# Forward substitution of the 16x16 triangular blocks issued by GpSimd (RWKV-7 + mLSTM hybrid layer)

## The chip, the cores and the metric

One core of a Trainium2 chip runs the whole program. Its engines are TensorE (PE, with its weight loads as PEld), VectorE (DVE), ScalarE (ACT), GpSimd (POOL) and SyncE (SP); each takes its instructions strictly in program order and waits at the head of its own queue until the semaphores of that instruction are there. The metric is the device time of one execution in microseconds, as the median of several runs.

## What is computed

One inference step of a decoder layer: RMSNorm, one projection `u @ w_in`, an RWKV-7 branch and an mLSTM branch on it, a gated merge, an output projection and a squared-ReLU MLP. 1024 new prompt tokens (with 16 meta tokens ahead of them, 1040 rows) and 8 running sequences of 8 tokens each go through it. The part that matters here is the RWKV-7 recurrence over 8 heads of width 64:

```python
def _rwkv7_step(S, inp):
    r, w, k, v, kk, a = inp
    sa = jnp.einsum('bhvk,bhk->bhv', S, -kk)
    S = S * w[:, :, None, :] + sa[..., None] * (kk * a)[:, :, None, :] + v[..., None] * k[:, :, None, :]
    return S, jnp.einsum('bhvk,bhk->bhv', S, r)
...
    S_T, y = lax.scan(_rwkv7_step, S0.astype(F32), (tm(r), tm(decay), tm(k), tm(v), tm(kk), tm(a)))
```

The kernel does it in chunks of 64 tokens. Within a chunk the step written with `sa` becomes a unit lower triangular 64x64 system for each head, and its inverse is needed. The inverse is built from the diagonal 16x16 blocks outwards: those blocks are inverted by forward substitution, and the blocks beside the diagonal follow by small matmuls.

## The kernel before

The program runs in stages. From about 85 to 880 us of the span it is in the RWKV stage: 24 steps (4 pairs of heads j, 6 groups g of 3 chunks). One step works on 2 heads x 64 tokens = 128 partitions and 3 chunks. A step is cut into four stages, and the program is pipelined over the steps: while stage a of step i runs, stage b of step i-1, stage c of step i-2 and stage d of step i-3 run beside it.

- Stage a makes the decays and the chunk matrices: rho (L654 to L656), `wa` and the running sum of log decays `cc` (L669, L672), products on GpSimd (L673, L684 to L687: RB and the middle part of KB), `bda` on VectorE (L682), the chunk matmuls L697, their masking X1 (L699), and the diagonal blocks `nd` (L703, L705). `nd` goes through DRAM to the tile NR by two DMAs (L709), which lays the 16x16 blocks out by row.
- Stage b starts with the forward substitution. L754 sets x to the identity; then, for n = 15 down to 1, L757 makes tmp = NR column * x column and L759 adds it to the remaining columns: 30 elementwise instructions of 128x3xn elements, each needing the one before it. L761 spreads x into the block diagonal XC, L764 transposes it, and the matmuls L769 to L798 with their evictions follow; L801 (ScalarE) and L802 (VectorE) write the result ATb.
- Stage c carries the state: L811, L814 and L815 (PE) read ATb, L822 and L823 make GH, L826 and L827 make MR, and then chunk after chunk PE's L885 (c = GH x Vs) and VectorE's L893 (next Vs = decay * c) wait for each other; L841 makes the outputs. One step of six also has the sample part (L853 to L923).
- Stage d is the group norm of the outputs (L938 to L953; L613 is on GpSimd, `newton`, L173 to L181, on VectorE).

Between the stages' matmuls PE runs filler: the projection matmuls L277, L279 and L281 of `Block.run`, 72 of them for each unit, which `pull(n)` places at points of a table. The tables (ORDER, ORDER_A, ORDER_B: stage letter, matmuls to pull) fix what `run_step` records. PE's order is kept as recorded (`manual_schedule`); the order of VectorE, ScalarE and GpSimd in this stage is set by the scheduler of the framework when the program is built, so it changes when instructions are given to another engine. The filler's weights are split in two parts: ScalarE casts `hi` (L199) and GpSimd makes `lo` = raw - hi (L201, 128x1024).

Of the kernel before, what the change touches and what calls it, by code (L numbers as in the profile page):

```python
# [12 lines left out]
ALU = mybir.AluOpType  # L13
# [16 lines left out]
G = 3  # L30
# [71 lines left out]
def tile_hybrid_trunk_step(ctx, tc, x_prompt, x_sample, st_S, st_shift, st_C, st_n, st_m, st_conv,  # L102
# [23 lines left out]
    def bank(nm):  # L126
        return PS["pool"].tile([128, 512], F32, tag=nm, name=nm, bufs=PS[nm])
# [20 lines left out]
    V = nc.vector  # L148
    PO = nc.gpsimd
# [5 lines left out]
    K = {k: (Cl[:, a:a + n] if k in LATE else Ct[:, a - NL:a - NL + n]) for k, (a, n) in OFF.items()}  # L155
# [213 lines left out]
    with banks(s=4, m=2), ExitStack() as st:  # L369
# [7 lines left out]
        for i in range(9):  # L377
            xt = xp.tile([128, D], F32, tag="xt", name="xt", bufs=9)
            n = 128 if i < 8 else 80
# [236 lines left out]
    def tl(n, sh=(GC,), bufs=1):  # L616
        return gp.tile([128] + list(sh), F32, tag=n, name=n, bufs=bufs)

    def hmm(o, l, r_, **kw):
        for s in HP:  # L620
            mm(o[s], lhsT=l[s], rhs=r_[s], **kw)
# [128 lines left out]
    def stage_b(j, g, st):  # L750
        X1, NR = st["X1"], st["NR"]
        x = tl("x", (G, 16))
        tmp = tl("tmp", (G, 16))
        V.tensor_copy(out=x, in_=K["xi"].unsqueeze(1).broadcast_to([128, G, 16]))  # L754
        for s in range(15):
            n = 15 - s
            V.tensor_tensor(out=tmp[:, :, :n], in0=NR[:, s + 1:16, :, s].rearrange("p t c -> p c t"),  # L757
                            in1=x[:, :, s:s + 1].broadcast_to([128, G, n]), op=ALU.mult)
            V.tensor_tensor(out=x[:, :, s + 1:16], in0=x[:, :, s + 1:16], in1=tmp[:, :, :n], op=ALU.add)  # L759
        XC, QC, XT = tl("XC", (G, 64)), tl("QC", (G * 32,)), tl("XT", (G, 64))  # L760
        V.tensor_tensor(out=XC.rearrange("p c (b t) -> p c b t", b=4), in0=x.unsqueeze(2).broadcast_to([128, G, 4, 16]),  # L761
                        in1=K["m16"].rearrange("p (b t) -> p b t", b=4).unsqueeze(1).broadcast_to([128, G, 4, 16]), op=ALU.mult)
        odd = lambda ap: ap.rearrange("p (b d) -> p b d", d=32)[:, :, 16:]
        V.transpose(out=XT, in_=XC)  # L764
        yield
        ps = bank("b")
        for c in range(G):
            for s in HP:
                mm(ps[s, 32 * c:32 * c + 32], lhsT=X1[s, c, 128:192], rhs=odd(XC[s, c]), start=True, stop=True)  # L769
        p4 = lambda t_: t_.rearrange("p (c b d) -> p c b d", c=G, d=16)  # L770
        V.tensor_tensor(out=p4(QC), in0=p4(ps[:, :32 * G]), in1=odd(K["mw32"]).unsqueeze(1).broadcast_to([128, G, 2, 16]), op=ALU.mult)
        yield
        ps = bank("b")
        for c in range(G):
            hmm(ps[:, 32 * c:32 * c + 32], XT[:, c], QC[:, 32 * c:32 * c + 32], start=True, stop=True)
        xv = XC.rearrange("p c (b d) -> p c b d", d=32)[:, :, :, 16:]
        V.tensor_tensor(out=xv, in0=p4(ps[:, :32 * G]), in1=xv, op=ALU.add)
        V.transpose(out=XT, in_=XC)
        for h, s in enumerate(HP):
            nc.scalar.copy(out=bd["x"][s, :, h, :], in_=XC[s])  # L780
        yield
        ps = bank("b")
        for c in range(G):
            for s, q in zip(HP, HQ):
                mm(ps[q, 32 * c:32 * c + 32], lhsT=X1[s, c, 128:160], rhs=XC[s, c, 32:], start=True, stop=True)
        for i, q in enumerate(HQ):
            V.tensor_copy(out=QZ[q], in_=ps[q, :32 * G])
        yield
        ps = bank("b")
        for c in range(G):  # L790
            for s, q in zip(HP, HQ):
                mm(ps[q, 32 * c:32 * c + 32], lhsT=XT[s, c, :32], rhs=QZ[s, 32 * c:32 * c + 32], start=True, stop=True)
        for h, q in enumerate(HQ):
            V.tensor_copy(out=bd["x"][q, :, h, 32:], in_=ps[q, :32 * G].rearrange("p (c d) -> p c d", c=G))
        yield
        ps = bank("b")
        for c in range(G):
            mm(ps[:, 128 * c:128 * c + 128], lhsT=flat(bd["x"][:, c]), rhs=X1[:, c, 0:128], start=True, stop=True)  # L798
        pv = ps[:, :128 * G].rearrange("p (c a t) -> p c a t", c=G, a=2)
        at = ATb.rearrange("p c a h t -> p c (a h) t")  # L800
        nc.scalar.copy(out=at[HP[0], :, 0::3], in_=pv[HP[0]])  # L801
        V.tensor_copy(out=at[HP[1], :, 1:3], in_=pv[HP[1]])  # L802
        yield
# [179 lines left out]
    for i in range(NS + 3):  # L983
        gens = {}
        for x, f, d in (("d", stage_d, 3), ("c", stage_c, 2), ("b", stage_b, 1)):
            if 0 <= i - d < NS:
                k = steps[i - d]
                gens[x] = f(*k, sts[k], SS_) if x == "c" else f(*k, sts[k])
        if i >= NS:
            run_step(gens, ORDER, 72 * (i < NS + 2), i == NS + 1)  # L990
            continue
        j, g = steps[i]
        if g == 0 and j:
            mix_all()
            queue.pop(0)
            run_step(gens, ORDER, 72)
            blocks(0)
            mix_all()
            queue.pop(0)
            run_step({"a": stage_a(j, g, sts[j, g])}, ORDER_A, 72 * FILLS[0])  # L1000
        else:
            gens["a"] = stage_a(j, g, sts[j, g])
            run_step(gens, ORDER_A if i == 0 else ORDER_B if i == 1 else ORDER, 72 * (FILLS[g] + (g == 5) * (1 if j == 3 else 2)), g == 1 and j > 0)
            while g == 5 and j < 3 and (live or queue[0]):
                pull(1)
                drain()
# [139 lines left out]
    for a, n in U_TILES:  # L1146
# [4 lines left out]
        for r_, T_, c in ((0, IG, 0), (32, FG, 1)):  # L1151
# [22 lines left out]
                    in1=MT[:, 15:15 + SEQ].rearrange("p (c t) -> p c t", t=128)[:, :, 0:1].broadcast_to([4, 8, 128]), op=ALU.add)  # L1174
# [4 lines left out]
    for c0 in (0, 5):  # L1179
        ps = sbank()  # L1180
        for c in range(c0, c0 + 5):
            a, n = CH[c]
            nc.tensor.transpose(ps[:n, 68 * (c - c0):68 * (c - c0) + 68], E2[:, a:a + n], ident[:68, :68])
        for c in range(c0, c0 + 5):
            a, n = CH[c]
# [660 lines left out]
```

## Time and profile before

| | before |
|---|---|
| median of 3 runs | 2103.38 us (2100.62 to 2105.63) |
| profiled execution: span from first to last instruction | 2102.9 us (0.5 us under the median of the runs; its own device time is not listed apart) |
| mean granted TensorE clock | 0.971 |
| RWKV stage, 100 to 880 us: PE / DVE / ACT / POOL busy | 708.0 / 609.9 / 269.5 / 174.0 us of 780 |
| L757, L759, L754 on DVE, whole span | 97.5 + 81.5 + 4.2 us |

Busy time is the time in which an engine executes; waiting at a semaphore is not counted. A row of the timeline gives the start in us, the duration in us, engine, line, operation, output and inputs with their shapes, and in brackets the idle time ahead of it on its engine with what ended it. A row of grouped lines ends with busy us, mean ns of one, and idle us ahead of the group's instructions.

One round of six steps (one pair of heads) takes some 198 us; the six steps between 281.9 and 479.7 us take 26.6, 32.0, 27.6, 27.1, 35.05 and 49.45 us. They are called A to F below, in this order; the last two have more filler.

### The profile page before, as it was taken

What the parts mean: (1) busy time and instruction counts of PE and PEld (TensorE: products, weight loads), DVE (VectorE), ACT (ScalarE), POOL (GpSimd) and SP (SyncE); (2) the same over time, 40 slices, a digit from 0 to 9 for tenths busy, and PEclk for the clock granted to TensorE, in tenths of its full rate; (3) what the DMA queues carried; (4) which work ended last, traced back from release to release, by engine and by line L of the source; (5) the groups of instructions that cost most, each with busy time, mean ns of one, the idle gap of its engine ahead of it and who ended that gap; (6) DMA issues with size and microseconds to landing.
All of it is one profiled execution on the core that took longest, in us unless ns stands there. A gap on an engine that the chain in (4) does not pass through costs nothing.

```text
span 2102.9 us, 32130 instructions
## 1 busy us (share of the span) xinstructions
PE 1974.6 (94%) x12325; PEld 1788.6 (85%) x12325; DVE 1364.2 (65%) x3503; ACT 704.7 (34%) x1654; POOL 511.1 (24%) x392
## 2 busy tenths in 40 slices
PE   8989898999989899989899997999999999999996
PEld 8978788888888788889888886988889999998895
DVE  6478778877887888578776639624444444445447
ACT  7333333333334333254654323331112222222122
POOL 2322122212222222122432404221112212112125
PEclk9999999999999999999999999999999999999998
DMA  5221111212111112231656614211111111111114
GB/s 162 62 68 54 46 52 57 64 45 66 55 51 49 52 61 66 64 107 62 230 175 200 215 60 145 71 51 41 41 41 41 50 51 41 51 41 43 49 32 164
DMA packets 148491, 161.59 MB, mean 77 GB/s; under 512 B 20429, under 2 KB 121607, under 8 KB 148337
## 3 DMA queue, kind: packets, MB, share of 16 engines
q1 hardware_dynamic: 148336, 159.54, 23.7%
q8 instruction: 97, 1.59, 0.3%
q14 instruction: 58, 0.47, 0.1%
HBM read 121.98 MB, written 37.27 MB: 76 GB/s over the span
## 4 chain that ended last, share of the span: by engine, by line
PE 48%; DVE 12%; ACT 2%; DMA 2%; issue 2%; POOL 1%; DVEq 0%; SPq 0%; ACTq 0%; POOLq 0%
PE g L215 11%; PE g L213 11%; PE g L214 11%; PE g L281 2%; PE g L277 2%; PE g L279 2%; PE g L1719 1%; DVE acc L1097 1%; PE g L1619 1%; PE g L1621 1%; PE g L1620 1%; POOL gb L1549 1%; DVE tmp L757 1%; DVE nw L173 1%; DVE ACC L1775 1%
## 5 line engine op out<-in xcount | busy, mean ns | idle before, releaser
L201 POOL TENSOR_TENSOR lo<-raw,hi 128x1024 fp32r<-128x1024 f32 x116 | 280.4, 2422 | 1039.6 <-ACT hi L199 1033.5
L281 PE MATMUL g<-u,lo 128*128 128x414 f32 (+4 forms) x1120 | 388.6, 347 | 1.8 <-POOL lo L201 1.8
L277 PE MATMUL g<-u,hi 128*128 128x414 f32 (+4 forms) x1120 | 387.0, 346 | 2.0 <-ACT gst L527 1.1
L279 PE MATMUL g<-u,hi 128*128 128x414 f32 (+4 forms) x1120 | 386.3, 345 | 0.0
L215 PE MATMUL g<-mg,lo 128*128 128x384 f32 (+1 forms) x768 | 252.3, 328 | 0.0
L213 PE MATMUL g<-mg,hi 128*128 128x384 f32 (+1 forms) x768 | 252.2, 328 | 0.0
L214 PE MATMUL g<-mg,hi 128*128 128x384 f32 (+1 forms) x768 | 252.1, 328 | 0.1
L199 ACT CAST hi<-raw 128x1024 fp32r<-128x1024 f32 x124 | 128.6, 1048 | 342.5 <-PE g L1719 250.9
L1755 DVE TENSOR_TENSOR ACC<-g,ACC 128x512 f32<-128x512 f32 x234 | 159.0, 689 | 111.2 <-PE g L215 105.1
L277 PEld LDWEIGHTS g<-u,hi 128*128 128x128 f32 x1120 | 219.4, 196 | 7.9 <-issue 1.5
L281 PEld LDWEIGHTS g<-u,lo 128*128 128x128 f32 x1120 | 219.6, 196 | 7.4 <-POOL lo L201 2.2
L279 PEld LDWEIGHTS g<-u,hi 128*128 128x128 f32 x1120 | 219.2, 196 | 4.3 <-issue 0.2
L213 PE MATMUL g<-hi,ah 128*128 128x512 f32 (+1 forms) x515 | 202.9, 394 | 0.0
L214 PE MATMUL g<-lo,ah 128*128 128x512 f32 (+1 forms) x515 | 202.7, 394 | 0.0
L215 PE MATMUL g<-hi,ah 128*128 128x512 f32 (+1 forms) x515 | 202.4, 393 | 0.0
L214 PEld LDWEIGHTS g<-mg,hi 128*128 128x128 f32 x768 | 144.6, 188 | 1.1 <-DVE mg L1594 0.4
L213 PEld LDWEIGHTS g<-mg,hi 128*128 128x128 f32 x768 | 144.7, 188 | 0.6
L215 PEld LDWEIGHTS g<-mg,lo 128*128 128x128 f32 x768 | 144.7, 188 | 0.0
L215 PEld LDWEIGHTS g<-hi,ah 128*128 128x128 f32 x515 | 96.7, 188 | 23.0
L213 PEld LDWEIGHTS g<-hi,ah 128*128 128x128 f32 x515 | 96.6, 188 | 22.3
L214 PEld LDWEIGHTS g<-lo,ah 128*128 128x128 f32 x515 | 96.7, 188 | 22.0
L757 DVE TENSOR_TENSOR tmp<-NR,x 128x45 f32<-128x45 f32 (+4 forms) x360 | 97.5, 271 | 20.8 <-DMA NR<-ndr 13.2
(852 smaller groups left out, 3609.3 us busy)
## 6 DMA issues: line engine op xcount, KB each, us to landing
raw<-in_w_in_dram SPq DMA_DIRECT2D x44, 512.0 KB
raw<-in_w_ff_up_dram SPq DMA_DIRECT2D x32, 512.0 KB
raw<-in_w_ff_down_dram SPq DMA_DIRECT2D x32, 512.0 KB
NR<-ndr SPq DMA_DIRECT2D x24, 384.0 KB
gscr<-gst SPq DMA_DIRECT2D x16, 544.0 KB
xt<-in_x_prompt_dram SPq DMA_DIRECT2D x15, 512.0 KB
ga<-gscr SPq DMA_DIRECT2D x8, 544.0 KB
pscr<-ga SPq DMA_DIRECT2D x8, 544.0 KB
```

The lines of the kernel that those rows point to most:

```text
L173: V.scalar_tensor_tensor(out=o, in0=a, scalar=c, in1=b, op0=f, op1=g)
L199: nc.scalar.copy(out=hi, in_=raw)
L201: (eng or PO).tensor_tensor(out=lo, in0=raw, in1=hi.bitcast(F32), op=ALU.subtract)
L213: mm(ps, lhsT=wh, rhs=xh, start=(i == 0), stop=False)
L214: mm(ps, lhsT=wh, rhs=xl, start=False, stop=False)
L215: mm(ps, lhsT=wl, rhs=xh, start=False, stop=(i == last))
L277: mm(ps, lhsT=hi[:, k], rhs=xh, start=(k == 0), stop=False)
L279: mm(ps, lhsT=hi[:, k], rhs=xl, start=False, stop=False)
L281: mm(ps, lhsT=lo[:, k], rhs=xh, start=False, stop=(k == 7))
L757: V.tensor_tensor(out=tmp[:, :, :n], in0=NR[:, s + 1:16, :, s].rearrange("p t c -> p c t"), in1=x[:, :, s:s + 1].broadcast_to([128, G, n]) ...
L1097: V.scalar_tensor_tensor(out=acc[:, a:a + m], in0=R[:, a + t_:a + t_ + m], scalar=cw(t_), in1=acc[:, a:a + m], op0=ALU.mult, op1=ALU.add)
L1755: V.tensor_tensor(out=ACC[:, i, cs], in0=ps, in1=ACC[:, i, cs], op=ALU.add)
```

## The change

The copy L754 and the 30 instructions of each forward substitution (L757, L759) are issued by GpSimd (`PO`) instead of VectorE (`V`): 24 copies and 720 elementwise instructions. What they compute, their tiles and the DMAs stay.

```diff
         x = tl("x", (G, 16))
         tmp = tl("tmp", (G, 16))
-        V.tensor_copy(out=x, in_=K["xi"].unsqueeze(1).broadcast_to([128, G, 16]))
+        PO.tensor_copy(out=x, in_=K["xi"].unsqueeze(1).broadcast_to([128, G, 16]))
         for s in range(15):
             n = 15 - s
-            V.tensor_tensor(out=tmp[:, :, :n], in0=NR[:, s + 1:16, :, s].rearrange("p t c -> p c t"),
-                            in1=x[:, :, s:s + 1].broadcast_to([128, G, n]), op=ALU.mult)
-            V.tensor_tensor(out=x[:, :, s + 1:16], in0=x[:, :, s + 1:16], in1=tmp[:, :, :n], op=ALU.add)
+            PO.tensor_tensor(out=tmp[:, :, :n], in0=NR[:, s + 1:16, :, s].rearrange("p t c -> p c t"),
+                             in1=x[:, :, s:s + 1].broadcast_to([128, G, n]), op=ALU.mult)
+            PO.tensor_tensor(out=x[:, :, s + 1:16], in0=x[:, :, s + 1:16], in1=tmp[:, :, :n], op=ALU.add)
```

PE's order is the same in both programs. VectorE's is not. The rows below are its order in step C, from the later half of the forward substitution to the first L893 of the step, before the change (`Ct` stands for a constant, x2 for two in a row):

```order
L656 RECIPROCAL rho<-rho 128x3
L759 TENSOR_TENSOR x<-x,tmp 128x3x11
L757 TENSOR_TENSOR tmp<-NR,x 128x3x10
L759 TENSOR_TENSOR x<-x,tmp 128x3x10
L757 TENSOR_TENSOR tmp<-NR,x 128x3x9
L759 TENSOR_TENSOR x<-x,tmp 128x3x9
L893 TENSOR_SCALAR Vs<-c,lam 64x65 x2
L757 TENSOR_TENSOR tmp<-NR,x 128x3x8
L669 TENSOR_SCALAR wa<-wa 128x384
```

L893 stands in the middle of the substitution, and L761, which uses its result, comes 16 further substitution instructions later. With the change the same place on VectorE reads:

```order
L822 TENSOR_TENSOR GH<-s,Ct 64x3x64 x2
L826 TENSOR_TENSOR MR<-s,RB_735 64x3x64 x2
L761 TENSOR_TENSOR XC<-x,Ct 128x192
L827 TENSOR_TENSOR MR<-s,Ct 64x3x64 x2
L654 TENSOR_SCALAR rho<-a 64x2
L655 TENSOR_SCALAR rho<-a 64x1
L654 TENSOR_SCALAR rho<-a 64x2
L655 TENSOR_SCALAR rho<-a 64x1
L764 STREAM_TRANSPOSE XT<-XC 128x192
L656 RECIPROCAL rho<-rho 128x3
L893 TENSOR_SCALAR Vs<-c,lam 64x65 x2
L669 TENSOR_SCALAR wa<-wa 128x384
```

L761 has moved ahead of L827, rho and L893. In step B (VectorE, with the change) it has moved ahead of the eviction L802 as well, whose ATb stage c's first matmul L811 reads:

```order
L952 SCALAR_TENSOR_TENSOR yo<-yo,PRM,bv 128x192
L953 TENSOR_TENSOR yo<-yo,gg 128x192
L625 TENSOR_TENSOR MB<-a,Ct 128x3x64
L761 TENSOR_TENSOR XC<-x,Ct 128x192
L764 STREAM_TRANSPOSE XT<-XC 128x192
L802 COPY ATb<-b 64x3x128
L740 TENSOR_TENSOR bv<-a,Zv 128x192
L822 TENSOR_TENSOR GH<-s,Ct 64x3x64 x2
```

Before, L802 of this step stood between two of the substitution's instructions, and L761 came behind L893's predecessors L822, L826 and L827.

On GpSimd, step C with the change has the substitution with one weight split L201 in it; these are the rows around that:

```order
L759 TENSOR_TENSOR x<-x,tmp 128x3x11
L757 TENSOR_TENSOR tmp<-NR,x 128x3x10
L759 TENSOR_TENSOR x<-x,tmp 128x3x10
L201 TENSOR_TENSOR lo<-raw,hi 128x1024
L757 TENSOR_TENSOR tmp<-NR,x 128x3x9
L759 TENSOR_TENSOR x<-x,tmp 128x3x9
```

GpSimd's other work of the step (L613, L673, L684 to L687) stands behind the last L759 and the copy L754.

## The prediction

> **What bounds the kernel now.** I read the span and the busy shares first, then stretches of it, then the waits, then the timeline of one step.
>
> ```profile
> span 2102.9 us, 32130 instructions
> PE 1974.6 (94%) x12325; PEld 1788.6 (85%) x12325; DVE 1364.2 (65%) x3503; ACT 704.7 (34%) x1654; POOL 511.1 (24%) x392
> ...
> 100.00:880.00 780.00, 708.03 (x5444) 643.84 (x5443) 609.92 (x2097) 269.53 (x740) 173.97 (x197) 0.95 0.19 58
> 1340.00:2050.00 710.00, 710.00 (x3682) 641.77 (x3681) 323.64 (x447) 156.22 (x260) 146.01 (x61) 1.00 0.14 44
> ```
>
> The last two rows are stretches (length, then busy PE, PEld, DVE, ACT, POOL, then the granted clock). The MLP (1340 to 2050) is PE from end to end. The RWKV stage (100 to 880) leaves PE idle for 72 us of 780, with DVE at 78% and POOL at 22%. So PE sets the end; elsewhere the change touches nothing. In this stage PE's order is fixed, and what counts is how long PE stands at an instruction that waits for DVE.
>
> ```profile
> PE c L885 <- DVE Vs L893: 47.0, 27, 2.6
> ...
> 347.29 0.24 DVE L757 TENSOR_TENSOR tmp<-NR,x 128x45 f32<-128x45 f32 x1 [0.37 <-DMA NR<-ndr]
> 354.56 0.72 DVE L827 TENSOR_TENSOR MR<-s,Ct 64x192 f32<-64x192 f32 x2
> 355.31 0.15 DVE L654 TENSOR_SCALAR rho<-a 64x2 f32<-64x2 f32 x1
> 356.13 0.17 DVE L656 RECIPROCAL rho<-rho 128x3 f32<-128x3 f32 x1
> 357.39 0.58 DVE L893 TENSOR_SCALAR Vs<-c,lam 64x65 f32<-64x65 f32 x2
> 365.24 0.36 DVE L761 TENSOR_TENSOR XC<-x,Ct 128x192 f32<-128x192 f32 x1
> 365.63 0.38 DVE L764 STREAM_TRANSPOSE XT<-XC 128x192 f32<-128x192 f32 x1
> ...
> 355.46 0.34 PE L277 MATMUL g<-u,hi 128*128 128x398 f32 x1
> 358.03 0.49 PE L885 MATMUL c<-Vs,GH 128*64 128x65 f32 x4 [2.23 <-DVE Vs L893]
> 359.49 0.55 PE L277 MATMUL g<-u,hi 128*128 128x414 f32 x1
> 361.51 0.36 PE L277 MATMUL g<-u,hi 128*128 128x414 f32 x1
> ```
>
> This is step C. PE's last filler starts at 355.46, then PE waits 2.23 us until DVE has done L893 at 357.39. So DVE is late already, by the substitution work around it. After such a stall matmuls take 0.55 instead of 0.36 us for some eight instructions: about 1.2 us more. Whatever delays L893 delays PE at once.
>
> **The change: what leaves DVE.**
>
> ```profile
> L757 DVE TENSOR_TENSOR tmp<-NR,x 128x45 f32<-128x45 f32 (+4 forms) x360 | 97.5, 271 | 20.8 <-DMA NR<-ndr 13.2
> L759 DVE TENSOR_TENSOR x<-x,tmp 128x45 f32<-128x45 f32 (+4 forms) x360 | 81.5, 226 | 7.6
> L754 DVE COPY x<-Ct 128x48 f32<-128x48 f32 x24 | 4.2, 177 | 0.1
> ```
>
> 97.5 + 81.5 + 4.2 = 183 us of DVE, 7.6 us a step. Alone that would shorten the 47.0 us of waits. But the changed order on DVE (shown with the change) puts L761, the reader of the finished substitution, ahead of L893, of rho and in some steps of L802. DVE stands at L761 until POOL has done all 30 instructions. The price on POOL decides.
>
> **The price on POOL.** No row shows a small strided tensor_tensor there. The nearest:
>
> ```profile
> L613 POOL TENSOR_TENSOR yo<-sqd,nt 128x128 fp32r<-128x128 f32 x4 | 1.9, 466 | 11.7 <-DVE tmp L757 9.5 <-PE a L697 2.2
> L685 POOL TENSOR_TENSOR wa<-wa,Zk 128x192 f32<-128x192 f32 x24 | 14.5, 605 | 0.7
> L835 POOL MEMSET Vs<- 64x65 f32 x8 | 1.2, 148 | 21.3 <-PE s L841 21.1
> L583 POOL MEMSET CVB<- 64x1 f32 x2 | 0.2, 92 | 0.1
> ...
> 163.26 0.58 POOL L685 TENSOR_TENSOR wa<-wa,Zk 128x192 f32<-128x192 f32 x1
> 163.92 0.60 POOL L686 TENSOR_TENSOR KB<-wa,li 128x192 f32<-128x192 f32 x1
> ```
>
> 128 elements take 466 ns and 192 take 605: 139 ns for 64 elements, 2.18 ns each, which leaves 466 - 128 x 2.18 = 186 ns fixed. L686 needs L685's result and starts 0.66 us after it: 0.08 us of gap. The substitution has 2 x 3 x (15 + ... + 1) = 720 elements in 30 instructions: 30 x 0.186 + 720 x 0.00218 + 30 x 0.08 = 5.6 + 1.6 + 2.4 = **9.6 us**. Bounds: at the price of the smallest MEMSET 30 x (0.092 + 0.08) = 5.2 us; at that of L835 6.8 us; at the unreduced 466 ns 30 x 0.546 = 16.4 us. I take 9.6, the line through the rows of the same operation.
>
> ```profile
> 376.03 2.35 POOL L201 TENSOR_TENSOR lo<-raw,hi 128x1024 fp32r<-128x1024 f32 x1 [13.62 <-ACT hi L199]
> 376.07 2.37 DVE L757 TENSOR_TENSOR tmp<-NR,x 128x42 f32<-128x42 f32 x1
> ```
>
> Two more terms. One L201 (2.35 us) stands inside the substitution on POOL in steps C, D and E, and in A ahead of it: 2.4 us. And a two-input DVE instruction beside a POOL one is held until that ends (L757 2.37 us against 0.2): POOL will be held in turn by DVE's instructions of 0.36 us, of which some three to four fall beside the substitution before DVE reaches L761: 1.0 us, estimated; 1.5 in B and F, where DVE has more to do.
>
> [...]
>
> **The sum, step by step.** In C the substitution starts at 347.29: 347.29 + 9.6 + 2.4 + 1.0 = 360.3. Then DVE does L761 0.36, L827 0.72, the four rho rows 0.62 (each 0.15 or 0.16), L764 0.38 and L656 0.17, so L893 starts at 360.3 + 2.25 = 362.5 instead of 357.39: PE loses **5.1 us** more. The other steps of the round:
>
> ```profile
> 288.60 2.37 POOL L201 TENSOR_TENSOR lo<-raw,hi 128x1024 fp32r<-128x1024 f32 x1 [9.24 <-ACT hi L199]
> 302.08 0.42 DVE L860 TENSOR_TENSOR smpG<-s,Ct 128x256 f32<-128x256 f32 x1
> ...
> 315.07 0.23 DVE L757 TENSOR_TENSOR tmp<-NR,x 128x45 f32<-128x45 f32 x1 [0.35 <-DMA NR<-ndr]
> 319.97 0.56 DVE L802 COPY ATb<-b 64x384 f32<-64x384 f32 x1
> 330.53 0.34 PE L885 MATMUL c<-Vs,GH 128*64 128x65 f32 x4 [2.60 <-DVE Vs L893]
> ...
> 375.49 0.23 DVE L757 TENSOR_TENSOR tmp<-NR,x 128x45 f32<-128x45 f32 x1
> 384.67 0.58 DVE L893 TENSOR_SCALAR Vs<-c,lam 64x65 f32<-64x65 f32 x2
> ...
> 401.60 0.23 DVE L757 TENSOR_TENSOR tmp<-NR,x 128x45 f32<-128x45 f32 x1 [0.20 <-DMA NR<-ndr]
> 414.26 0.58 DVE L893 TENSOR_SCALAR Vs<-c,lam 64x65 f32<-64x65 f32 x2
> 421.45 0.34 PE L885 MATMUL c<-Vs,GH 128*64 128x65 f32 x4 [2.46 <-DVE Vs L893]
> ...
> 437.11 0.23 DVE L757 TENSOR_TENSOR tmp<-NR,x 128x45 f32<-128x45 f32 x1 [1.49 <-DMA NR<-ndr]
> 442.27 0.56 DVE L802 COPY ATb<-b 64x384 f32<-64x384 f32 x1
> 448.35 0.67 PE L885 MATMUL c<-Vs,GH 128*64 128x65 f32 x4 [1.64 <-ACT GH L823]
> ```
>
> - A: L201 ends at 290.97; + 9.6 + one more product inside (L855, 128x256, taken at L685's 0.6) + 1.0 = 302.2. Between L761 and L860, whose result PE's L871 waits for, DVE has eight or nine instructions of about 0.4 (L761, L672, L764, L680, two of L682 and others), some 3.4 us: 305.6 against 302.08, **+3.5**.
> - B: 315.07 + 11.1 = 326.2; with L761 and L764 0.74, L802 starts at 326.9 against 319.97, +6.9, and PE's L811, which now starts 0.4 after L802's end, is late by 6.5. DVE is then free for L893, so the old stall of 2.60 and its 1.2 of slower matmuls go (6.5 - 3.8): **+2.7**.
> - D: NR can be read at 375.49 at the latest (DVE was busy until then; I assume 0.6 earlier): 374.9 + 13.0 + L761, rho, L764, L656 1.53 = 389.4 against 384.67, **+4.8**.
> - E: 401.60 + 13.0 + 2.25 = 416.9 against 414.26, +2.6; the later stall of 2.46 goes for the most part: **+0.5**.
> - F: 437.11 + 11.1 + L761 and L952 0.8 = 449.0 against 442.27, +6.7; a stall of 1.6 behind it and the 1.2 of slower matmuls are spared: **+3.8**.
>
> Sum 3.5 + 2.7 + 5.1 + 4.8 + 0.5 + 3.8 = 20.4 us a round, x 4 rounds = 82. Two more long stalls a round with 1.2 us of slower matmuls each: + 10. So 2102.9 + 92 = **2195 us**; the profiled execution lies 0.5 us under the median of the runs, so the sum stands for that as well. One us more or less in the substitution is worth about 22 us.
>
> The copy L754 costs POOL some 0.3 us (by the same line) behind L761; POOL's idle time hides it. L673 to L686 come behind it on POOL; but L673 needs cc, which DVE makes behind L893 and which is as late as PE is, and their reader L697 moves with PE's own delay, so I add nothing. If that cover is gone, each step pays part of the five instructions' 3 us (5 x 0.605).
>
> **Rivals.**
> - *Faster, by a cheap POOL.* If an instruction costs about 0.17 us with its gap (5.2 us a step), C gains nothing (347.29 + 5.2 + 3.4 + 2.25 = 358.1 against 357.39), but B, E and F lose their old stalls; with a third of the 47.0 us of waits gone, 2102.9 - 16 = 2087. It decides from 6 us of substitution downwards. For: MEMSET at 92 ns. Against: two operands and 186 ns by the line. Chance 0.09.
> - *Dearer.* At 16.4 us, 6.8 more in each of 24 steps: 2195 + 163 = 2358. A milder form: every DVE instruction in flight holds POOL, seven times 0.36 instead of three, + 1.5 x 22 = 2228. Chance of 2230 and over 0.2.
> - *Nothing is seen.* PE's filler covers the wait: 2103. Against: PE's order is fixed, and the filler ahead of L885 already ends 2.23 us too soon. Chance 0.05.
> - The instructions do move in the order of the changed program, so that nothing moves isn't one.
>
> **How the numbers follow.** The forecast's mechanism at 6.8 to 12 us has 0.66, and with the dear form slower has 0.86. Its low end is 6.8 us: 2195 - 2.8 x 22 = 2133. To take in part of the cheap case the range goes down to 2105, upwards to 2320 (15 us of substitution); 0.09 lies below, 0.05 above. A measurement of this kernel tells 0.2% (4 us) from no change: faster 0.09, same 0.05, slower 0.86.
>
> **What would show it.** Right: L757 and L759 on POOL at 190 to 290 ns, first to last of a step 10 to 13 us; a new wait of DVE's L761 for POOL's L759, 24 times; waits of PE at L885, L811 and L871 for DVE well over 47 us; no change after 880. Wrong: POOL's pitch under 0.2 us; L893 not later against L757; or POOL's records at 0.5 us and over.

## The result, and the profile after

The changed kernel takes 2201.11 us (median of 4 runs, 2197.49 to 2201.62) against 2104.51 us of the kernel before in the same measurement: a ratio of 1.0455, 95% interval 1.0438 to 1.0472. The forecast was 2195 us, with a range of 2105 to 2320. The change makes the kernel slower by 97 us.

The page of the changed kernel begins:

```profile
span 2199.3 us, 32140 instructions
## 1 busy us (share of the span) xinstructions
PE 2000.9 (91%) x12325; PEld 1812.3 (82%) x12325; DVE 1216.0 (55%) x2759; ACT 705.8 (32%) x1654; POOL 691.8 (31%) x1136
...
PEclk9988898889989998899999999999999999999998
```

DVE's busy time falls by 148 us and POOL's rises by 181. (The rows that left DVE add up to 183 us; DVE's records overlap, and the page counts an overlapping stretch once: 1475.4 us of records are 1364.2 us of busy time before, 1291.7 are 1216.0 now.) PE does the same 12325 matmuls, but is busy for 26.3 us more (2000.9 - 1974.6) and idle for 70.1 us more (198.4 against 128.3): together the 96.4 us of the span. The granted clock has its eights in slices 3 to 17, which are the RWKV stage, and in the last slice, where the kernel before has one too. Behind the last L953, where the stage ends, both kernels need the same time (1218.7 us before, 1219.5 now): the whole loss lies in the stage.

The groups of the substitution on POOL (count, busy us, mean ns, idle us ahead):

```profile
L757 POOL TENSOR_TENSOR tmp<-NR,x 128x45 f32<-128x45 f32 (+4 forms) x360 | 89.9, 250 | 232.8 <-DMA NR<-ndr 207.3
L759 POOL TENSOR_TENSOR x<-x,tmp 128x45 f32<-128x45 f32 (+4 forms) x360 | 86.6, 240 | 27.1
```

Without the waits for NR (207.3 of the 232.8 us ahead of L757, which leaves 25.5) the 24 substitutions take 89.9 + 86.6 + 25.5 + 27.1 = 229.1 us, 9.55 us each. The forecast had 9.6.

The waits of the changed kernel (us in total, times, longest):

```profile
DVE XC L761 <- POOL x L759: 170.1, 24, 9.0
...
PE c L885 <- DVE Vs L893: 74.9, 15, 7.0
PE s L811 <- DVE ATb L802: 34.5, 6, 6.2
PE c L869 <- POOL wa L673: 9.9, 3, 4.0
PE c L871 <- DVE smpG L860: 8.0, 3, 2.7
```

The first row is the new wait: in each of the 24 steps DVE stands at L761, 7.1 us on the mean. The next four are PE's longest waits in the stage, 127.3 us together; before, L885 had 47.0 us and L811 0.9. Step C of the same round shows how the one becomes the other (timeline of POOL, DVE and PE together):

```profile
380.50 0.49 POOL L757 TENSOR_TENSOR tmp<-NR,x 128x45 f32<-128x45 f32 x1 [7.73 <-DMA NR<-ndr]
381.07 0.28 POOL L759 TENSOR_TENSOR x<-x,tmp 128x45 f32<-128x45 f32 x1
...
388.50 0.34 PE L277 MATMUL g<-u,hi 128*128 128x398 f32 x1
...
392.00 0.20 POOL L757 TENSOR_TENSOR tmp<-NR,x 128x3 f32<-128x3 f32 x1
392.28 0.20 POOL L759 TENSOR_TENSOR x<-x,tmp 128x3 f32<-128x3 f32 x1
392.51 0.36 DVE L761 TENSOR_TENSOR XC<-x,Ct 128x192 f32<-128x192 f32 x1 [8.00 <-POOL x L759]
392.90 0.72 DVE L827 TENSOR_TENSOR MR<-s,Ct 64x192 f32<-64x192 f32 x2
...
394.68 0.58 DVE L893 TENSOR_SCALAR Vs<-c,lam 64x65 f32<-64x65 f32 x2
395.32 0.49 PE L885 MATMUL c<-Vs,GH 128*64 128x65 f32 x4 [6.49 <-DVE Vs L893]
```

The substitution runs from 380.50 to 392.48, with one split L201 in it. DVE idles for 8.00 us at L761; from there to L893 it needs 2.17 us (forecast 2.25), and PE, whose filler ended at 388.84, has stood for 6.49 us. L893 comes 14.2 us after the first L757; before it came 10.1 us after it (357.39 - 347.29).

### The profile page after: what moved, and what is told of

Its sections match the earlier page's. It is cut to its first block, busy times and chain, and to the rows that moved or that the text cites. A ratio compares the mean times of both kernels' runs of the same rounds, so it can differ in the third digit from the quotient of the medians.

```text
span 2199.3 us, 32140 instructions
## 1 busy us (share of the span) xinstructions
PE 2000.9 (91%) x12325; PEld 1812.3 (82%) x12325; DVE 1216.0 (55%) x2759; ACT 705.8 (32%) x1654; POOL 691.8 (31%) x1136
## 4 chain that ended last, share of the span: by engine, by line
PE 47%; DVE 9%; POOL 4%; DMA 3%; issue 2%; ACT 2%; DVEq 0%; SPq 0%; POOLq 0%; ACTq 0%
PE g L215 11%; PE g L213 11%; PE g L214 11%; PE g L281 2%; PE g L277 2%; PE g L279 2%; PE g L1719 1%; DMA NR<-ndr 1%; POOL tmp L757 1%; POOL x L759 1%; PE g L1619 1%; PE g L1621 1%; PE g L1620 1%; POOL gb L1549 1%; DVE nw L173 1%
## 5 line engine op out<-in xcount | busy, mean ns | idle before, releaser
L201 POOL TENSOR_TENSOR lo<-raw,hi 128x1024 fp32r<-128x1024 f32 x116 | 280.4, 2422 | 783.0 <-ACT hi L199 777.0
L277 PE MATMUL g<-u,hi 128*128 128x414 f32 (+4 forms) x1120 | 392.1, 350 | 3.6 <-ACT gst L527 2.8
L281 PE MATMUL g<-u,lo 128*128 128x414 f32 (+4 forms) x1120 | 393.1, 351 | 1.4 <-POOL lo L201 1.4
L279 PE MATMUL g<-u,hi 128*128 128x414 f32 (+4 forms) x1120 | 390.0, 348 | 0.0
L277 PEld LDWEIGHTS g<-u,hi 128*128 128x128 f32 x1120 | 223.3, 199 | 9.7 <-ACT gst L527 3.2
L279 PEld LDWEIGHTS g<-u,hi 128*128 128x128 f32 x1120 | 223.1, 199 | 4.4 <-issue 0.2
L757 POOL TENSOR_TENSOR tmp<-NR,x 128x45 f32<-128x45 f32 (+4 forms) x360 | 89.9, 250 | 232.8 <-DMA NR<-ndr 207.3
```

Source lines behind the costliest of these rows:

```text
L201: (eng or PO).tensor_tensor(out=lo, in0=raw, in1=hi.bitcast(F32), op=ALU.subtract)
L277: mm(ps, lhsT=hi[:, k], rhs=xh, start=(k == 0), stop=False)
L279: mm(ps, lhsT=hi[:, k], rhs=xl, start=False, stop=False)
L281: mm(ps, lhsT=lo[:, k], rhs=xh, start=False, stop=(k == 7))
L757: PO.tensor_tensor(out=tmp[:, :, :n], in0=NR[:, s + 1:16, :, s].rearrange("p t c -> p c t"), in1=x[:, :, s:s + 1].broadcast_to([128, G, n] ...
```

## The experiments

Two theories stood against each other. **Theory 1**, the forecast's: the loss is made by DVE's queue, in which L761 stands ahead of L893 and L802, so that the length of the substitution on POOL is paid by PE. **Theory 2**: POOL itself is the bound; its products L673 to L686 stand behind the substitution, and L697 waits for them. (A third, that the two engines hold each other up while both run, is taken up with the first run.)

### L761 pinned where it was recorded

`tc.keep_in_program_order` keeps an instruction behind all that is recorded ahead of it on its engine.

```diff
-        V.tensor_tensor(out=XC.rearrange("p c (b t) -> p c b t", b=4), ...
+        tc.keep_in_program_order(V.tensor_tensor(out=XC.rearrange("p c (b t) -> p c b t", b=4), ...
```

> The change, with L761 pinned on VectorE behind what is recorded ahead of it (L802, L826, L827, rho and the first L893 of the step); L672 (cc) and the second L893 still stand behind it. Theory 1 (the loss is VectorE standing at L761 in its queue, with L893 and L802 behind it): most of the 97 us goes, 2095 to 2130 us, and the waits of PE at L885 and L811 for VectorE (75 + 35 us with the change) fall under 50. Theory 2 (the loss is GpSimd itself: the substitution delays its products L673 to L686, and so L697): the time stays within 15 us of 2201. Theory 3 (shared access of both engines slows both): stays as well.

2132.41 us, ratio to before 1.0135 (1.0106 to 1.0163), just above the expected range. 69 of the 97 us are gone, though all 24 x 31 instructions are still on POOL. The waits at L811 are gone; those at L885 are 54.3 us, a little over the expected 50, since cc and the second L893 still stand behind L761 (in step C, L761 comes at 365.73 after 5.21 us of waiting, that L893 at 368.33). Theories 2 and 3 expected no difference.

### L761 pinned behind all L893

```diff
-        XC, QC, XT = tl("XC", (G, 64)), ...
+        yield; XC, QC, XT = tl("XC", (G, 64)), ...
...
-    ORDER = (... ('c', 9), ('d', 1), ('a', 0), ('b', 8), ...
+    ORDER = (... ('c', 9), ('b', 0), ('d', 1), ('a', 0), ('b', 8), ...
```

(with the pin of the run before, and one more `('b', 0)` in ORDER_B). PE's order stays.

> The change, with L761 and L764 recorded later in the step, ahead of the matmuls L697, and L761 pinned on VectorE behind all L893 of the step. Theory 1: the stalls of PE for L893 and L802 go, VectorE is also free of 183 us of work: 2060 to 2095 us, faster than before the change. Theory 2: L686 and so L697 stay late, 2150 to 2200. If GpSimd finishes the substitution after PE's L769 wants XC, PE waits there instead: 2105 to 2150 with new waits at L769.

2090.18 us, ratio 0.9933 (0.9911 to 0.9956): 0.7% under the kernel before, a small gain but clear of its interval. Its waits, and the place in step C where the next one is made:

```profile
PE a L697 <- POOL KB L686: 21.8, 12, 3.4
PE c L871 <- DVE smpG L860: 15.9, 3, 5.4
PE c L885 <- DVE Vs L893: 7.8, 3, 5.0
```

```profile
352.92 0.56 DVE L672 TENSOR_TENSOR_SCAN cc<-Ct,wa 128x192 f32<-128x192 f32 x1
...
357.96 0.20 POOL L759 TENSOR_TENSOR x<-x,tmp 128x3 f32<-128x3 f32 x1
358.53 0.60 POOL L673 TENSOR_TENSOR wa<-cc,wa 128x192 f32<-128x192 f32 x1
361.05 0.58 POOL L686 TENSOR_TENSOR KB<-wa,li 128x192 f32<-128x192 f32 x1
361.68 1.24 PE L697 MATMUL a<-KB,bda 128*128 128x192 f32 x6 [2.07 <-POOL KB L686]
```

The waits for L893 have fallen from 74.9 to 7.8 us. Now theory 2 has its turn: cc is done at 353.48, but L673 stands behind the substitution until 358.53, and L697 waits for L686. It was no part of the loss of the change: there POOL itself waits for cc at L673 (70.2 us, in 20 of the 24 steps), and the last row of the table below shows that taking the products off POOL gains nothing there. It is the next bound.

### That bound taken away, and each half alone

The four products of L673, L684, L685 and L686 go to DVE:

```diff
-        PO.tensor_tensor(out=tw, in0=cc, in1=tw, op=ALU.subtract)
+        V.tensor_tensor(out=tw, in0=cc, in1=tw, op=ALU.subtract)
...
-        PO.tensor_scalar(out=ta, in0=ta, scalar1=pc(P_KA), ...
-        PO.tensor_tensor(out=ta, in0=ta, in1=zk, op=ALU.mult)
-        PO.tensor_tensor(out=KB[:, :, 1, :], in0=g3(ta), ...
+        V.tensor_scalar(out=ta, in0=ta, scalar1=pc(P_KA), ...
+        V.tensor_tensor(out=ta, in0=ta, in1=zk, op=ALU.mult)
+        V.tensor_tensor(out=KB[:, :, 1, :], in0=g3(ta), ...
```

once on the pinned kernel, once on the kernel before, once on the changed kernel without a pin.

> As e3_pin_late, and the four products L673, L684, L685, L686, which stand behind the substitution on GpSimd there (L697 waits 22 us for L686, L871 16 us for work behind L673), are issued by VectorE, which is idle at that place. If GpSimd's order is what bounds e3_pin_late: those waits go, with slower matmuls behind them, 2030 to 2065 us. If VectorE has no room for them: 2085 us and over.

> The kernel before with only the four products L673, L684, L685, L686 moved from GpSimd to VectorE, the substitution left on VectorE. It tells whether a gain of e6_products is that of the products alone: with VectorE at 78% in this stage, 24 x 4 x 0.36 = 35 us more on it: 2110 to 2135 us. If the products on GpSimd were a bound of their own: under 2100.

> The change with the four products L673, L684, L685, L686 on VectorE, and no pin: L761 still stands ahead of L893 and L802. If the place of L761 is what costs (theory 1), the products' move alone gains little here, since cc and all behind it still wait for L761: 2180 to 2205 us. If the products on GpSimd behind the substitution were the cause (theory 2): under 2120.

| kernel | us | ratio to before (95%) |
|---|---|---|
| pinned late, products on DVE | 2021.67 | 0.9598 (0.9578 to 0.9618) |
| before, products on DVE | 2105.61 | 1.0005 (0.9990 to 1.0020) |
| changed, products on DVE, no pin | 2206.19 | 1.0454 (1.0409 to 1.0499) |

The first beats both kernels, by 4.0% and 8.2%, and more than expected. Neither half does it alone: the products' move is worth nothing on the kernel before (which was expected to become slower; DVE had the room, as PE's waits for L893 are 43.6 us there against 47.0) and nothing while L761 stands ahead of L893 (waits at L885 77.7 us and at L811 32.7, as in the changed kernel). The page and the waits of the best kernel:

```profile
span 2018.9 us, 32130 instructions
## 1 busy us (share of the span) xinstructions
PE 1945.4 (96%) x12325; PEld 1767.3 (88%) x12325; DVE 1240.1 (61%) x2855; ACT 707.1 (35%) x1654; POOL 645.8 (32%) x1040
```

```profile
DVE XC L761 <- POOL x L759: 16.2, 11, 6.6
...
PE b L769 <- DVE XC L761: 5.8, 4, 4.2
PE a L697 <- DVE KB L686: 5.8, 3, 1.9
```

PE is idle for 73.5 us of the span (2018.9 - 1945.4) instead of 128.3, and its busy time is 29 us shorter than before.

### The length of the substitution

```diff
-        for s in range(15):
+        for s in range(10):
```

> The change with the last 5 of the 15 rounds of the substitution left out (20 instructions instead of 30, the short ones gone), so the result isn't the reference's. Theory 1: the substitution takes 2.9 us less (10 x 0.266 + 90 x 0.00218), worth 22 us for each: 2201 - 64 = 2137 us, 2125 to 2155. If instead the loss goes with the number of instructions alone, a third of 97 us: 2169.

This leaves out the last five of the fifteen rounds. 2145.89 us, 55 us less than the changed kernel. The substitutions took 6.5 us instead of 9.5, so one microsecond is worth 18 us of the whole, against 22 in the forecast.

### No substitution at all

```diff
-        for s in range(15):
+        for s in range(0):
```

in the kernel before, which leaves out all 30 instructions and keeps the copy.

> The kernel before with the 30 instructions of each substitution left out (the copy L754 stays on VectorE), so the result isn't the reference's; it prices what a freed VectorE is worth. Theory 1: the waits of PE for L893 (47 us) go mostly, with the slower matmuls behind them: 2045 to 2087 us. If VectorE's load is no matter in this stage: 2100 to 2105.

2018.95 us, ratio 0.9589 (0.9569 to 0.9608): 87 us under the kernel before, more than expected. PE is idle for 53 us less (45 of them at L893, where 2.0 of the 47.0 us are left) and busy for 33 us less. So the substitution on DVE cost the kernel before some 87 us, and the best kernel above, at 2021.67 us, hides it nearly whole.

### The split L201 off POOL

```diff
-                self.w = wload(kxm(w_in[0], self.c0, 128), 8, 128)
+                self.w = wload(kxm(w_in[0], self.c0, 128), 8, 128, eng=V)
```

> The change with the weight split L201 of the projection's blocks (w_in) on VectorE, so that none stands inside a substitution on GpSimd any more; L761 still stands ahead of L893. Prediction's term: 2.4 us in 13 of 24 steps, 31 us less: 2165 to 2180 us, if the split's time on VectorE (some 1.2 us a unit) falls into its idle time; if it doesn't, 2180 to 2200. If the split inside the substitution did not count: 2195 to 2210.

> As e6_products, with the split L201 of the w_in blocks on VectorE as well, so that GpSimd runs the substitution without it. e6_products has 16 us of waits of VectorE at L761 left: if the split inside the substitution makes them, 2005 to 2018 us; if VectorE now gets too much, 2022 to 2045.

On the changed kernel: 2171.30 us, the 30 us expected. But the substitution of step C became only 1.6 us shorter (10.39 against 11.98 us), as one of its own instructions now runs long beside a split on DVE (L759, at 370.71, takes 1.12 us; the split runs from 370.42 to 371.71); all 24 substitutions together became 18 us shorter, not 31. The time agrees with the term of 2.4 us, but the term isn't confirmed: between the two profiled executions (32.5 us apart) PE stands 25 us less (L885 58.0 instead of 74.9, L811 30.5 instead of 34.5) and is busy 8 us less. On the best kernel: 2017.59 us, ratio 0.9564 (0.9528 to 0.9601), not told apart from 2021.67, though DVE's waits at L761 fall from 16.2 to 8.9 us.

### The copy alone back on DVE

```diff
-        PO.tensor_copy(out=x, in_=K["xi"].unsqueeze(1).broadcast_to([128, G, 16]))
+        V.tensor_copy(out=x, in_=K["xi"].unsqueeze(1).broadcast_to([128, G, 16]))
```

> The change with the copy L754 alone back on VectorE. By the prediction the copy is hidden on GpSimd: no difference from the changed kernel, 2197 to 2205 us. If it counts on GpSimd's path (0.25 us before L673 in each step): up to 6 us faster.

2219.99 us, ratio 1.0538 (1.0516 to 1.0560): a miss, 19 us slower than the changed kernel. Step B of the changed kernel, POOL and DVE:

```profile
355.27 0.36 DVE L761 TENSOR_TENSOR XC<-x,Ct 128x192 f32<-128x192 f32 x1 [6.19 <-POOL x L759]
355.69 0.22 POOL L754 COPY x<-Ct 128x48 f32<-128x48 f32 x1 [0.46 <-DVE XC L761]
355.87 2.35 POOL L201 TENSOR_TENSOR lo<-raw,hi 128x1024 fp32r<-128x1024 f32 x1
```

and of this run:

```profile
358.39 0.20 POOL L759 TENSOR_TENSOR x<-x,tmp 128x3 f32<-128x3 f32 x1
358.55 2.34 POOL L201 TENSOR_TENSOR lo<-raw,hi 128x1024 fp32r<-128x1024 f32 x1
358.62 2.48 DVE L761 TENSOR_TENSOR XC<-x,Ct 128x192 f32<-128x192 f32 x1 [6.17 <-POOL x L759]
```

On POOL the copy has to wait for L761, and so keeps the split behind it from starting. Without it the split starts 0.07 us ahead of L761, which then takes 2.48 us instead of 0.36, and PE's wait at L811 grows from 5.29 to 7.49 us. All waits at L811 grow by 11.6 us (34.5 to 46.1) and those at L885 by 6.5 (74.9 to 81.4): 18 of the 19 us. In step C, a part of the latter is the copy itself, 0.17 us ahead of L893 on DVE, and L761 takes 0.60 us there instead of 0.36.

## Why the prediction was right

- *The price on POOL* (9.6 us by the line through L613 and L685, 0.186 us fixed and 0.08 us between): 9.55 us. The shortest instructions take 0.20 us at a pitch of 0.28 (392.00 to 392.28 above). The line held down to 3 elements, and both bounds, 5.2 and 16.4 us, were far off.
- *The place of L761.* Shown by the pins: with the same work on the same engines and the same order on PE, L761 ahead of L893 and L802 gives 2201 us, behind the first L893 2132, behind all of them 2090.
- *The steps.* PE's idle time from one first L757 to the next, before and after, in this round: A 1.5 to 5.6 us (forecast of the difference +3.5), B 3.3 to 6.0 (+2.7), C 2.5 to 6.5 (+5.1), D 2.3 to 6.0 (+4.8), E 3.3 to 2.8 (+0.5), F 3.5 to 8.0 (+3.8). The sum of the differences is 18.5 us against 20.4. The two aren't quite the same thing: the forecast's B and F also take off 1.2 us each of slower matmuls, so its idle time alone is 22.8 us (and F's own terms add up to 3.9). B's agreement is therefore chance: its idle time was forecast at 3.9. C and D were forecast too high by the 1.0 us for POOL being held by DVE: in step C the substitution takes 9.6 us net of the split, so next to nothing holds POOL while DVE stands at L761. Where DVE does work beside it (pinned late), a substitution takes 10.0 us net of other work, so the term is about 0.5 us there. The reading behind the term was too wide as well: before the change 14 of the substitution's instructions that ran beside an L201 took 1.38 to 2.38 us and ended 0.04 to 0.06 us behind it, but L740, which has two inputs too, took 0.36 us beside one (at 177.25).
- *The slower matmuls* were sized too small: 10 us, less the 10 that B and F had taken off in four rounds, so nothing net; measured 26.3 us of PE's busy time. The count was not far off (gaps of PE of over 2 us in the stage went from 17 to 28, 11 more where the forecast had 8); the price of each was. By the granted clock in the traces PE works under half the clock for 99.5 us of the span before, 159.5 in the changed kernel and 48.4 in the best one. In the traces before and after, the filler's matmuls of 414 columns start every 0.346 us under half the clock and every 0.189 us under the full one (medians). At that pitch 0.45 of the time is lost, by estimate 45 us before, 72 in the changed kernel and 22 in the best one: 27 us more than before in the changed kernel, about the whole difference of 26.3 us, and 23 us less in the best one, most of the 29 us that it gains.
- So the two terms erred in opposite ways (idle time 22.8 x 4 = 91 against 70 us, slower matmuls nothing net against 26), and that the sum of 92 us met 97 so closely is luck. The mechanism and the price on POOL are not.
- *Nothing is seen* and *the dearer POOL* are refuted by the time and by the 240 to 250 ns. *The faster rival* didn't come about, as POOL wasn't that cheap. Its size was too small: a substitution of no length gains 87 us, where the rival had 16 at 5.2 us. It counted a third of the waits at L885 (the run without the substitution frees 45 of 47.0 us) and left out the 33 us of slower matmuls.
- *The signs* held: 250 and 240 ns, 9.8 to 12.9 us from first to last in all 24 steps, a new wait at L761 24 times, and 117 us of waits at L885, L811 and L871.
- *The copy at nothing* holds for where the change has it. That its wait shields L761 from L201 I hadn't seen.

## What to carry to other kernels

When work goes to another engine, look first where its reader stands in the queue of the engine that is freed: here DVE stood 7.1 us a step at L761 with L893 and L802 behind it, and PE's waits for those two rose from 47.9 to 109.4 us. The scheduler may put the reader early, as it did here (why it did is not shown). Pin the reader behind what the critical engine waits for, and then look what now stands behind the moved work on its new engine. Here the same move was 4.5% slower as the scheduler ordered it, and 4.0% faster with the reader pinned and four products moved the other way.

## What the hardware showed besides

Stretches of the changed kernel's step C (length, busy PE, PEld, DVE, ACT, POOL, granted clock, DMA share, GB/s), around the stall of 6.49 us that begins at 388.84, and then:

```profile
388.14:391.55 3.41, 0.70 (x4) 0.37 (x3) 0.00 (x0) 0.00 (x0) 2.54 (x12) 1.00 0.55 154
391.55:394.97 3.42, 0.00 (x0) 0.00 (x0) 2.32 (x10) 0.00 (x0) 1.32 (x6) 0.50 0.00 0
394.97:398.38 3.41, 3.06 (x15) 2.88 (x16) 3.14 (x8) 1.57 (x5) 1.90 (x4) 0.50 0.00 0
398.40:402.00 3.60, 3.60 (x29) 3.24 (x29) 1.75 (x5) 1.42 (x4) 1.24 (x2) 1.00 0.01 2
```

And of the kernel before, two stretches each around a stall of 1.84 us (277.03 to 278.87), the stall of 2.23 us in step C, and one of 2.59 us in the last round (721.46 to 724.05). The row behind them is the matmul that ends the last of these stalls:

```profile
276.12:279.53 3.41, 1.57 (x9) 1.22 (x9) 2.15 (x4) 2.20 (x7) 3.16 (x6) 1.00 0.02 5
279.53:282.94 3.41, 3.41 (x13) 3.12 (x12) 1.95 (x6) 0.55 (x2) 0.00 (x0) 0.50 0.03 6
354.63:358.04 3.41, 1.18 (x9) 0.85 (x7) 3.11 (x17) 0.00 (x0) 0.00 (x0) 1.00 0.30 90
358.04:361.45 3.41, 3.41 (x16) 3.22 (x17) 3.31 (x14) 2.08 (x6) 2.25 (x4) 0.50 0.00 0
719.85:723.27 3.42, 1.61 (x9) 1.28 (x7) 3.10 (x17) 0.00 (x0) 0.00 (x0) 1.00 0.03 10
723.27:726.68 3.41, 2.63 (x16) 2.34 (x16) 3.15 (x11) 1.50 (x5) 1.45 (x3) 1.00 0.01 2
```

```profile
724.05 0.34 PE L885 MATMUL c<-Vs,GH 128*64 128x65 f32 x4 [2.59 <-DVE Vs L893]
```

In the RWKV stage of these two traces half the clock is granted in stretches of 3.41 us or whole multiples of it (6.83, 10.24 and 13.65). In the kernel before 19 of 21 such stretches last 3.41 us; in the changed kernel 23 of 26 last 6.83 us or more, as in step C above: half the clock is granted from 391.55 on, 2.71 us into the stall of 6.49 us, and PE's 3.06 us of work up to 398.38 run under it too. In these rows the length of a stall alone does not tell what follows: half the clock comes behind the stalls of 1.84 and 2.23 us and not behind the one of 2.59 us. That one is split over the two stretches printed for it, and PE works for 1.61 and 2.63 us in them; in the stretches ahead of the half clock it works for 1.57, 1.18 and 0.70 us. What decides it is not shown: half the clock is also granted from 300.0 to 303.4 us of the kernel before, with no stall of PE of over 1.45 us in the 10 us ahead of it.

A small elementwise instruction costs little more on POOL than on DVE here (L757 250 against 271 ns on the mean, where DVE's mean holds seven instructions of over 2 us, each of which ran beside an L201 on POOL and ended 0.04 to 0.06 us behind it; 239 against 198 ns for the median, 0.20 against 0.17 us for the instructions of 128x3), while at 192 elements the product L685 takes 0.605 us on POOL and 0.36 on DVE in the best kernel.
